# Where in the program a modulation's loads and sums are emitted: in the recurrence's chunks, or between projections and gates

## The chip, the cores and the metric

The kernel runs on one core of a Trainium2 chip. The metric is the time of one execution on the device in microseconds (us); of each kernel several runs are timed and the median counts. Five engines work side by side, each through its own queue and strictly in that queue's order: PE (TensorE, matrix products), DVE (VectorE), ACT (ScalarE), POOL (GpSimd) and SP (SyncE, which here only issues loads and stores). They wait for one another through semaphores. An instruction that waits holds up everything behind it on its own engine, and on no other.

## The reference, cut to what matters

One layer of a conditioned decoder for 512 tokens of 1024 channels, in float32:

```python
mod = c @ ada_w + ada_b                       # c: 1024 values, ada_w: 1024 x 6144
sh1, sc1, g1, sh2, sc2, g2 = split(mod, 6)
h = rmsnorm(x) * (1 + sc1) + sh1
z = h @ w_in                                  # -> attention | RWKV-7 | convolution | 3 gates
o_attn, o_rwkv, o_conv = attention(z_attn), rwkv7(z_rwkv), gated_conv(z_conv)
merged = sum(sigmoid(z_gate[i]) * (o[i] @ w_branch[i]) for i in range(3))
x = x + g1 * (merged @ w_o)
h = rmsnorm(x) * (1 + sc2) + sh2
x = x + g2 * ffn(h)
return rmsnorm(x)
```

The attention picks 128 keys for every query by an indexer's scores. The RWKV branch is a recurrence over tokens. Of the modulation, `sh1` and `sc1` are needed at once, for `h`. The other four parts, `g1`, `sh2`, `sc2` and `g2`, are needed only after `merged`: they are what is moved here.

## The kernel before, in words

**Products.** `h` is kept with channels on partitions, as a pair of parts (`h_hi`, `h_lo`). The columns of `w_in` are taken 128 at a time (`z_col`, line 402). Each such block is a load of 512 KB by SP (`load_raw`, L147, tile `wraw`, 4 buffers), a copy of its high part by ACT (`whi`, L163), the rest by POOL (`wlo`, L165; 3 buffers of each), and then 24 matmuls on PE (lines 177 to 179, below called column products) into one of three PSUM banks called `mm`. All 512 tokens run through each matmul. The RWKV branch has 14 of these blocks, 5 of them done early, the convolution 12, the attention 13 and then products with tokens on partitions (L188 to L190), the gates 24.

**The RWKV branch.** After its columns are there, four pairs of heads are prepared (L457 to L554; the last products on PE are those of L544 and L553). Then comes the substitution (L562 to L579): DVE alone inverts small triangular matrices in 31 steps, each a multiply (L569) and an add (L571) that needs the multiply. The matrices come in by the load `sub<-blk`, and the result goes through DRAM (`blk<-sub`, then four loads `Dm<-blk`, issued by ACT), is transposed by DVE (L579) and used by PE (L588, L591). Then the recurrence: 8 chunks of 64 tokens in turn (L602 to L650), a chain PE, DVE, PE, ACT, PE. Then a norm per head (L656 to L663, DVE), products that turn the result (L669), and the output of the branch.

**The rest up to the merge.** The convolution, the projections of the attention with the relative bias (masks `mk` on DVE, L721, products L727), the indexer's scores and the selection on DVE (L839 and L840, 32 rounds for each block of queries), the masked softmax for four pairs of heads (L855 to L897), and three branches of gates and branch products (`branch`, line 911). Then `w_o`, the second norm and the feed-forward part, which this change does not touch.

**The moved work.** `ada_parts` (line 196) is a Python generator. Each step loads one block of `ada_w` of 256 KB (tile `xraw`, three buffers) and adds it, times a column of `c`, to the tile `acc` on DVE: L215 for the first of eight blocks, L217 for the other seven. `finish` (line 199) sums a complete `acc` over the partitions with four one-column matmuls (L202) into an `mm` bank, and adds `ada_b` on DVE (L203). There are 64 steps in 8 groups of 8, and a last one that only finishes.

**What sets the order.** A tile framework with a scheduler writes the queue of each engine. It starts from the order in which the Python code emits the instructions, lets each engine run ahead by its own estimate of when operands are there, and respects the buffers. It may so place an instruction well before or after the place at which it was emitted. `with tc.high_priority` pulls the `whi` and `wlo` work forward. Memory comes from pools stacked from the left and from the right; a pool opened in a place used before waits, tile by tile, for the former users.

Of the kernel before, what the change touches and what calls it, by code (L numbers as in the profile page):

```python
# [19 lines left out]
D, S, MIX, DFF = 1024, 512, 512, 2816  # L20
# [39 lines left out]
def hybrid_block(ctx, tc, ins, out, consts, dbg=None, stop=99):  # L60
# [36 lines left out]
    start = right_pool("start")  # L97
# [52 lines left out]
    def weights(name, base, ld, k0, kt, cols, own=None, raw_own=None):  # L150
        """Rows 128*k0.. (kt blocks) and the columns [(start, width)..] of a row-major matrix with row length ld,
        as a pair of float32r tiles [128, kt, width] whose sum is the matrix."""
        wid = sum(n for _, n in cols)
        srcs, o = [], 0
        for c, n in cols:
            srcs.append(((lambda r, o=o, n=n: r[:, :, o:o + n]),
                         dram(name, base + k0 * 128 * ld + c, [[ld, 128], [128 * ld, kt], [1, n]])))
            o += n
        raw = load_raw([128, kt, wid], srcs, raw_own)
        pool, tag, bufs = (wp.pool, "w", 3) if own is None else (own[0], "x", own[1])  # L160
        with tc.high_priority(offset=4000):
            hi = pool.tile([128, kt, wid], F32R, name=tag + "hi", tag=tag + "hi", bufs=bufs)
            ACT.activation(hi, raw, AF.Copy)  # L163
            lo = pool.tile([128, kt, wid], F32R, name=tag + "lo", tag=tag + "lo", bufs=bufs)
            lo_engine[0].tensor_tensor(lo, raw, hi, op=ALU.subtract)  # L165
        return hi, lo
# [4 lines left out]
    def mm_t(ps, w, act, k0=0, start=True, stop=True):  # L171
        """ps += w^T @ act: the columns of w on partitions; act = (hi, lo) with channels on partitions."""
        hi, lo = w
        ahi, alo = act
        kt = hi.shape[1]
        for k in range(kt):
            PE.matmul(ps, hi[:, k, :], ahi[:, k0 + k, :], start=start and k == 0, stop=False)  # L177
            PE.matmul(ps, hi[:, k, :], alo[:, k0 + k, :], start=False, stop=False)  # L178
            PE.matmul(ps, lo[:, k, :], ahi[:, k0 + k, :], start=False, stop=stop and k == kt - 1)  # L179

    def mm_n(ps, act, tb, w, k0=0, start=True, stop=True):
        """ps += act^T @ w for the tokens of block tb (tokens on partitions)."""
# [13 lines left out]
    def ada_parts():  # L196
        """Parts 2.. of the modulation, half a part at a time: c_k * ada_w[k, 512 columns] summed over the eight row
        blocks, then over the partitions."""
# [28 lines left out]
    def rsqrt_of(v, n):  # L227
        """v^-1/2 of a small tile to full precision, in place: the table's root and one Newton step."""
        y = T("rsqt", [128, 32])[:, :n]
        ACT.activation(y, v, AF.Sqrt)  # L230
        DVE.reciprocal(y, y)
        DVE.scalar_tensor_tensor(v, v, -0.5, y, op0=ALU.mult, op1=ALU.mult)
        DVE.tensor_tensor(v, v, y, op=ALU.mult)
        DVE.scalar_tensor_tensor(v, v, 1.5, y, op0=ALU.add, op1=ALU.mult)
        return v

    def rsqrt_bits(v, n):
        """The same without a table: a first value from the bits of v, within 3.5 %, and three Newton steps, of which each
        squares the error."""
# [8 lines left out]
    def rstd_of(ss, n):  # L248
        """1/sqrt(ss/D + eps), in place."""
# [7 lines left out]
    def ada_first(c0, n):  # L257
        """Chunks c0..c0+n of the first two parts of the modulation, not yet summed over partitions."""
# [88 lines left out]
    def rel_pos(name, shape, aps, pos0, pool, keep=None):  # L347
        """Positions less the first one, in float32: exact however large they are, as long as the differences are exact."""
# [11 lines left out]
    def bias_operands():  # L360
# [16 lines left out]
        # scaled by a power of two to magnitudes under 2^15, and split into two parts of 11 bits  # L377
# [42 lines left out]
    def mixed(dst, i):  # L420
        """dst = z + (shift(z) - z) * mu for column block i of the branch."""
# [6 lines left out]
    # every sigmoid here is (1 + tanh(x / 2)) / 2, from the table that holds the exponential, too; lora_g, cs, a hold  # L428
    # twice the sigmoid, its running sum, and the tanh

    # unit u = pair * 8 + chunk; rows 0-63 / 64-127: the two heads of a pair, or for tokens
    # (own half q) U, L, N_b, B and (other half z) V, M, N_k, K
# [24 lines left out]
    for p in range(4):  # L457
# [51 lines left out]
        # V with tokens on partitions  # L509
# [10 lines left out]
        # products within the chunks  # L520
# [25 lines left out]
        # B and K, decayed to the chunk's end, with tokens on partitions  # L546
# [8 lines left out]
    ep.close()  # L555

    # (I - L)^-1: 32x32 diagonal blocks by substitution, one block per partition
# [42 lines left out]
    # the chunks in turn  # L600
    S_ = None
    for c in range(8):  # L602
        if c:
# [47 lines left out]
    # group norm per head and token, back to channels on partitions  # L651
# [35 lines left out]
    def conv3(dst, src, wts):  # L687
        """dst[t] = src[t-2] w0 + src[t-1] w1 + src[t] w2 along the free axis."""
# [17 lines left out]
    adp = left_pool("adp")  # L706
# [35 lines left out]
    # q, k and the indexer's as float32r pairs; row r of a block holds its high part, then its low part  # L742
# [46 lines left out]
    # A product of two 64-row operands in two passes: [q_hi; q_lo] with [k_hi; k_hi], then q_hi with k_lo. Heads of odd  # L789
    # number have the halves of the first operand swapped, so that q_hi lies where k_lo does.  # L790
    def load_q(dst, z, t0, n):
        """dst [128, 2, n]: the two heads of block z, tokens t0.."""
# [53 lines left out]
    # pT holds the transposed probabilities of both heads: key block b of the first in row b from column (b + 1) * 128,  # L846
    # that of the second in row 3 - b up to column (4 - b) * 128
# [62 lines left out]
    # merged holds twice the sum  # L910
# [42 lines left out]
    op_.close()  # L953
    adp.close()
    cvp.close()
    mid.close()

# [7 lines left out]
    def row_bc(c0, pool):  # L965
        """Modulation columns c0.. of modc as a row of 1024 on every partition."""
# [19 lines left out]
    def residual(x, hf, bank, row, ss):  # L986
        """x += row * (what the bank holds), and the sum of squares of the new values."""
# [14 lines left out]
    # Block rows of W^T: columns of a, columns of g. Blocks of the inner dimension: k < 512, k >= 512. Block columns of  # L1002
    # h: the two halves of the tokens.
# [7 lines left out]
    def pair(shape, src, ring=None):  # L1011
        """src as a pair of float32r tiles."""
# [36 lines left out]
    def product(ps, w, b, first):  # L1049
        """ps += w^T b over 512 rows."""  # L1050
# [20 lines left out]
    def h_block(c, th, dst):  # L1071
        """dst = h of channel block c, token half th."""
# [133 lines left out]
    # Inner blocks: the even and the odd channel blocks of f, pair by pair. Rows: the two halves of the tokens; columns:  # L1206
    # the two halves of the channels. First sweep: four products, each in its own banks; second sweep: the other three on
    # top of those, of which copies are kept.
# [15 lines left out]
    def w_tile(n, srcs):  # L1224
        """float32r pair [128, n, 512] of the sources, which fill it in turn."""
# [26 lines left out]
    def down(ps, i, a, ai, w, wi, first=False, last=False):  # L1252
        """ps += a^T w for the tokens of block i of a half."""
# [63 lines left out]
    def add_g2(tb, hf, v):  # L1317
        """x += g2 * v, v a half row in two pieces."""
# [8 lines left out]
    def high_half(tb):  # L1327
        """The columns of the second half, complete but for the norm's factor."""
# [92 lines left out]
```

## Time and profile before

| what | value |
|---|---|
| median of 3 runs | 1248.59 us (1246.18 to 1259.89) |
| the profiled execution, first to last instruction | 1246.3 us |
| PE busy, of that span | 1076.5 us (86%) |
| DVE busy | 945.3 us (76%) |
| ACT, POOL busy | 495.6 and 522.9 us |

The page gives the span of the profiled execution and no second time around it; the span lies within the three runs, 2.3 us under their median. A matmul's end is modelled, so a PE that the profile calls busy may still have room; the distance between the starts of two matmuls in a row is the safer measure. The granted clock (PEclk) is TensorE's, as a share of its full 2.4 GHz: 1.00 is full speed, and a mean between 0.5 and 1 says that part of the stretch ran at the lower level of 1.2 GHz. A wait is put down to the releaser that came last.

### The profile page before, as it was taken

To read this page: it belongs to the slowest core of one execution; us is meant where nothing else is said; L and a number is where in the kernel's file an instruction comes from. 1 tells how busy PE (TensorE), PEld (TensorE's weight loads), DVE (VectorE), ACT (ScalarE), POOL (GpSimd) and SP (SyncE) were. 2 spreads that over 40 slices of the span, in tenths; PEclk is the share of its full clock that TensorE was granted. 3 is DMA by queue.
4 is the path that set the end of the run, shared out by engine and by line. 5 is a ranking of instruction groups with operands and counts; after the bars stand their busy time and mean duration, and the time that the engine had idled before them with its cause. 6 is when DMAs were issued, how large, how long until landed. Compare 5 with 4: busy or idle time off the path is not lost.

```text
span 1246.3 us, 18485 instructions
## 1 busy us (share of the span) xinstructions
PE 1076.5 (86%) x6896; PEld 871.0 (70%) x6896; DVE 945.3 (76%) x1538; ACT 495.6 (40%) x890; POOL 522.9 (42%) x372
## 2 busy tenths in 40 slices
PE   4798999799999799888989999989888887679665
PEld 3676678577667768665666788889888886557444
DVE  6778777532789378976655444899898898999997
ACT  4243422242434244223434333665445454444442
POOL 3232223322222415554541000156566565776762
PEclk9789999899989899988999999989999999899898
DMA  9632123412348933698653535312323232244611
GB/s 313 174 86 71 39 60 102 95 35 66 107 150 253 303 96 86 193 235 218 179 134 98 145 101 166 115 51 85 92 79 101 73 99 85 76 170 168 218 53 68
DMA packets 194247, 156.97 MB, mean 126 GB/s; under 512 B 18499, under 2 KB 167389, under 8 KB 194157
## 3 DMA queue, kind: packets, MB, share of 16 engines
q1 hardware_dynamic: 165773, 131.22, 36.1%
q10 hardware_dynamic: 23056, 14.53, 3.9%
q0 software_dynamic: 5328, 10.03, 3.6%
q8 instruction: 54, 0.88, 0.3%
q14 instruction: 36, 0.29, 0.1%
HBM read 137.13 MB, written 18.63 MB: 125 GB/s over the span
## 4 chain that ended last, share of the span: by engine, by line
PE 39%; DVE 37%; issue 10%; DMA 6%; ACT 4%; POOL 2%; SPq 0%; ACTq 0%; DVEq 0%; POOLq 0%
PE mm L177 6%; PE mm L179 6%; PE mm L178 6%; DVE wlo L1237 3%; DMA xraw<-in_ada_w 3%; DVE acc L217 2%; DVE mg_lo L1250 2%; DVE h_lo L1046 2%; DVE slo L1237 2%; DVE slo L1017 2%; DVE acc L271 2%; PE sd L801 2%; DVE sub L571 1%; PE sd L727 1%; PE sd L800 1%
## 5 line engine op out<-in xcount | busy, mean ns | idle before, releaser
L165 POOL TENSOR_TENSOR wlo<-wraw,whi 128x1024 fp32r<-128x1024 f32 (+1 forms) x70 | 154.2, 2204 | 279.8 <-ACT whi L163 225.7
L178 PE MATMUL mm<-h_lo,whi 128*128 128x512 f32 (+2 forms) x496 | 201.8, 407 | 1.2 <-DVE h_lo L1082 1.2
L177 PE MATMUL mm<-h_hi,whi 128*128 128x512 f32 (+2 forms) x496 | 202.1, 408 | 0.7 <-DVE o_cv L702 0.7
L179 PE MATMUL mm<-h_hi,wlo 128*128 128x512 f32 (+2 forms) x496 | 201.3, 406 | 0.0
L163 ACT ACTIVATE whi<-wraw 128x1024 fp32r<-128x1024 f32 (+1 forms) x86 | 80.1, 934 | 222.2 <-PE mm L178 91.8
L178 PEld LDWEIGHTS mm<-h_lo,whi 128*128 128x128 f32 (+1 forms) x496 | 95.7, 193 | 23.5 <-issue 2.5
L177 PEld LDWEIGHTS mm<-h_hi,whi 128*128 128x128 f32 (+1 forms) x496 | 95.4, 193 | 22.4 <-issue 3.2
L179 PEld LDWEIGHTS mm<-h_hi,wlo 128*128 128x128 f32 (+1 forms) x496 | 95.6, 193 | 21.4 <-issue 1.5
L1053 PE MATMUL sd<-mg_hi,shi 128*128 128x256 f32 x240 | 70.1, 292 | 18.0 <-DVE p L1185 17.8
L1034 POOL TENSOR_TENSOR fS<-wraw 128x512 f32<-128x512 f32 x20 | 29.8, 1490 | 129.2 <-DMA wraw<-in_ffn_w_up 125.6
L217 DVE SCALAR_TENSOR_TENSOR acc<-xraw,ccol,acc 128x512 f32<-128x512 f32 x56 | 60.5, 1080 | 23.0 <-DMA xraw<-in_ada_w 22.5
L1055 PE MATMUL sd<-mg_hi,slo 128*128 128x256 f32 x240 | 68.1, 284 | 0.0
L1054 PE MATMUL sd<-mg_lo,shi 128*128 128x256 f32 x240 | 68.0, 283 | 0.0
L1017 DVE TENSOR_TENSOR slo<-fS,shi 128x1024 fp32r<-128x1024 f32 x40 | 60.5, 1512 | 0.5 <-ACT shi L1016 0.4
L1053 PEld LDWEIGHTS sd<-mg_hi,shi 128*128 128x128 f32 x240 | 45.9, 191 | 21.1 <-DVE p L1185 21.1
L1017 DVE TENSOR_TENSOR wlo<-wraw,whi 128x1024 fp32r<-128x1024 f32 x27 | 34.0, 1260 | 20.2 <-ACT whi L1016 20.1
L1053 PE MATMUL mm<-h_hi,whi 128*128 128x256 f32 x160 | 46.1, 288 | 3.0 <-ACT p L1066 3.0
L721 DVE TENSOR_SCALAR mk<-posq,thr 128x512 f16<-128x512 f32 (+3 forms) x128 | 44.7, 421 | 4.1 <-PE sd L727 4.1
L1016 ACT ACTIVATE shi<-fS 128x1024 fp32r<-128x1024 f32 x40 | 42.1, 1052 | 10.7 <-PE sd L1054 10.5
L1054 PEld LDWEIGHTS sd<-mg_lo,shi 128*128 128x128 f32 x240 | 46.0, 192 | 0.0
L1055 PEld LDWEIGHTS sd<-mg_hi,slo 128*128 128x128 f32 x240 | 45.9, 191 | 0.0
L1054 PE MATMUL mm<-h_lo,whi 128*128 128x256 f32 x160 | 45.6, 285 | 0.0
(565 smaller groups left out, 3120.6 us busy)
## 6 DMA issues: line engine op xcount, KB each, us to landing
wraw<-in_w_in SPq DMA_DIRECT2D x61, 512.0 KB, 4.1
xraw<-in_ada_w SPq DMA_DIRECT2D x96, 256.0 KB, 4.2
wraw<-in_ffn_w_up SPq DMA_DIRECT2D x44, 512.0 KB, 3.8
wraw<-in_ffn_w_down SPq DMA_DIRECT2D x17, 512.0 KB, 3.5
wraw<-in_w_branch SPq DMA_DIRECT2D x24, 256.0 KB, 3.6
bias_d<-stage ACTq DMA_DIRECT2D x10, 512.0 KB, 5.8
wraw<-in_w_o SPq DMA_DIRECT2D x8, 512.0 KB, 3.8
h_hi<-in_ffn_w_down SPq DMA_DIRECT2D x8, 512.0 KB, 4.5
```

The lines of the kernel that those rows point to most:

```text
L163: ACT.activation(hi, raw, AF.Copy)
L165: lo_engine[0].tensor_tensor(lo, raw, hi, op=ALU.subtract)
L177: PE.matmul(ps, hi[:, k, :], ahi[:, k0 + k, :], start=start and k == 0, stop=False)
L178: PE.matmul(ps, hi[:, k, :], alo[:, k0 + k, :], start=False, stop=False)
L179: PE.matmul(ps, lo[:, k, :], ahi[:, k0 + k, :], start=False, stop=stop and k == kt - 1)
L217: DVE.scalar_tensor_tensor(acc, raw, ck, acc, op0=ALU.mult, op1=ALU.add)
L721: DVE.tensor_scalar(m_[:, :n], posq[:, b * 128:], thr[:, b, gg:gg + 1], None, op0=ALU.is_ge)
L1017: DVE.tensor_tensor(lo, src, hi, op=ALU.subtract)
L1053: PE.matmul(ps, at(w[0], k), b[0][:, k], start=first and k == 0, stop=False, skip_group_check=True)
L1054: PE.matmul(ps, at(w[0], k), b[1][:, k], start=False, stop=False, skip_group_check=True)
L1055: PE.matmul(ps, at(w[1], k), b[0][:, k], start=False, stop=k == 3, skip_group_check=True)
L1237: DVE.tensor_tensor(lo[:, d], src, hi[:, d], op=ALU.subtract)
```

## The change

Five steps of the generator are taken at the head of each of the 8 chunks, 40 of the 64, which before were taken in `branch`. The four steps between the attention's key projections stay, and `branch` takes what is left. So that the tiles exist, the pool `adp` is opened after the RWKV preparation instead of after the convolution, and closed after the convolution's pool instead of before it. Comments and docstrings are gone as well, which computes nothing and shifts line numbers by one to three from here on.

```diff
     ep.close()
+    adp = left_pool("adp")
     sp = right_pool("sp")
 ...
     S_ = None
     for c in range(8):
+        for _ in range(5):
+            next(ada)
         if c:
             px = sd_bank()
 ...
     tap("o_conv", o_cv)
-    adp = left_pool("adp")
     bi = right_pool("bi")
 ...
     mg.close()
     op_.close()
-    adp.close()
     cvp.close()
+    adp.close()
     mid.close()
```

What the scheduler makes of it is seen in the queues. First SP, from the loads of the recurrence's first weights on. `wraw` are column weights, `xraw` the modulation's blocks. Before:

```order
L147 DMA wraw<-in_w_in 128x8x128 x3
L373 DMA rb<-in_rel_bias 128x1x8
L374 DMA rb<-in_rel_bias 124x1x8
L147 DMA wraw<-in_w_in 128x8x128 x22
L147 DMA wraw<-in_w_in 128x8x72
L147 DMA wraw<-in_w_in 128x8x128 x3
L755 DMA z_att<-wk 128x512
```

And with the change:

```order
L374 DMA rb<-in_rel_bias 124x1x8
L147 DMA wraw<-in_w_in 128x8x128 x13
L147 DMA xraw<-in_ada_w 128x512 x44
L147 DMA wraw<-in_w_in 128x8x128
L147 DMA xraw<-in_ada_w 128x512 x4
L147 DMA wraw<-in_w_in 128x8x128
L147 DMA xraw<-in_ada_w 128x512 x3
L147 DMA wraw<-in_w_in 128x8x128 x7
L351 DMA posqi<-in_positions 128x512
```

Forty-four modulation loads now stand between the sixteenth and the seventeenth of the column weights, and seven more close behind.

Second, DVE at the start of the substitution. Before, between its steps stand operations of the convolution (L690 and others):

```order
L563 MEMSET sub 128x1024
L564 MEMSET sub 128x32
L569 TENSOR_TENSOR st<-sub 128x31
L698 TENSOR_TENSOR wk<-wk,mm 128x512
L571 TENSOR_TENSOR sub<-sub,st 128x31
L569 TENSOR_TENSOR st<-sub 128x60
L571 TENSOR_TENSOR sub<-sub,st 128x30x2
L569 TENSOR_TENSOR st<-sub 128x87
L690 SCALAR_TENSOR_TENSOR wk<-wk,cw 128x511
```

With the change (L570 and L572 are the multiply and the add):

```order
L564 MEMSET sub 128x1024
L565 MEMSET sub 128x32
L215 TENSOR_SCALAR acc<-xraw,ccol 128x512
L570 TENSOR_TENSOR st<-sub 128x31
L217 SCALAR_TENSOR_TENSOR acc<-xraw,ccol,acc 128x512
L572 TENSOR_TENSOR sub<-sub,st 128x31
L217 SCALAR_TENSOR_TENSOR acc<-xraw,ccol,acc 128x512
L570 TENSOR_TENSOR st<-sub 128x60
L572 TENSOR_TENSOR sub<-sub,st 128x30x2
L570 TENSOR_TENSOR st<-sub 128x87
L572 TENSOR_TENSOR sub<-sub,st 128x29x3
L217 SCALAR_TENSOR_TENSOR acc<-xraw,ccol,acc 128x512
```

It goes on like this: of the modulation's 64 sums, 38 stand among the 62 steps of the substitution and ten between its end and the last of the transposes L580. So the scheduler did not put them into the chunks, at whose heads they are emitted, but before them. The other 16 stand in the selection for the last block of queries; none stands in the softmax, which had 24 before.

Third, PE and ACT right behind the preparation of the last pair of heads. On PE before, column products follow at once; there are 183 of them from here to the first L588:

```order
L553 MATMUL sd<-ident,BK 128x128 x3
L544 MATMUL sd<-UV,LM 64x64 x7
L553 MATMUL sd<-ident,BK 128x128 x5
L179 MATMUL mm<-h_hi,wlo 128x512
L177 MATMUL mm<-h_hi,whi 128x512
```

With the change (buffer numbers kept), four `finish` of the modulation come first, and then 60 column products up to the first L589:

```order
L553 MATMUL sd_1459<-ident_70,BK_1302 128x128 x4
L202 MATMUL mm_1803<-one_66,acc_1691 128x1 x4
L202 MATMUL mm_1926<-one_66,acc_1741 128x1 x4
L202 MATMUL mm_2003<-one_66,acc_1864 128x1 x4
L202 MATMUL mm_2126<-one_66,acc_1941 128x1 x4
L177 MATMUL mm_2309<-h_hi_93,whi_2305 128x512
```

The fourth of them reads the `acc` that is complete with sum 32. On ACT, the store of the substitution's result, `blk<-sub`, now follows the load of its input directly, ahead of the next `whi`; before, five `whi` stood between the two:

```order
L554 ACTIVATE HYL<-sd 128x4x2x64 x2
L563 DMA sub<-blk 128x1024
L574 DMA blk<-sub 128x1024
L163 ACTIVATE whi<-wraw 128x1024
L699 ACTIVATE wk<-mm 128x512
L576 DMA Dm<-blk 32x32x32
```

In all of the program's queue on PE, the column products that stand ahead of some marks are, before and with the change: first L588/L589 416 and 276; first product of the head norm (L669/L672) 623 and 432; first product of the indexer (L821/L823) 816 and 816; first transposition of the softmax (L885/L887) 1185 and 1108; its last product (L894/L896) 1433 and 1331; all 1872 and 1872.

## Rows read from the trace of the kernel before

**Rows 1.** Windows: busy us (count) of each engine, granted clock, DMA share.
```profile
core 0: us, PE busy (x) PEld busy (x) DVE busy (x) ACT busy (x) POOL busy (x), PEclk, DMA share, GB/s
186.00:230.00 44.00, 42.89 (x183) 33.85 (x181) 35.25 (x67) 9.86 (x13) 14.90 (x6) 1.00 0.31 85
237.00:247.00 10.00, 10.00 (x36) 7.74 (x34) 4.86 (x4) 1.06 (x1) 4.62 (x2) 0.74 0.57 122
256.00:312.00 56.00, 55.53 (x607) 43.25 (x602) 18.66 (x37) 16.75 (x35) 12.25 (x10) 1.00 0.19 54
341.00:425.00 84.00, 79.73 (x928) 62.35 (x926) 68.91 (x160) 30.16 (x60) 26.26 (x16) 0.96 0.77 226
425.00:441.00 16.00, 11.40 (x80) 11.11 (x81) 0.75 (x1) 3.74 (x5) 5.73 (x4) 0.79 0.98 240
441.00:548.00 107.00, 100.82 (x416) 75.20 (x415) 98.68 (x200) 38.53 (x66) 52.31 (x35) 0.97 0.49 140
548.00:688.00 140.00, 124.64 (x531) 88.13 (x530) 81.58 (x185) 53.07 (x127) 56.62 (x45) 0.94 0.66 164
688.00:745.00 57.00, 57.00 (x249) 46.10 (x248) 26.55 (x35) 21.34 (x30) 2.94 (x4) 1.00 0.47 128
```

**Rows 2.** Groups by line, DVE, 191 to 232: busy, mean ns, idle before.
```profile
L571 DVE TENSOR_TENSOR sub<-sub,st 128x31 f32<-128x31 f32 (+15 forms) x31 | 19.0, 614 | 0.9
L569 DVE TENSOR_TENSOR st<-sub 128x31 f32<-128x31 f32 (+15 forms) x31 | 10.6, 341 | 6.6 <-DMA sub<-blk 5.7
```

**Rows 3.** Timeline (start us, us), POOL and DVE in the substitution.
```profile
199.35 0.30 DVE L571 TENSOR_TENSOR sub<-sub,st 128x135 f32<-128x135 f32 x1
...
199.79 2.47 POOL L165 TENSOR_TENSOR wlo<-wraw,whi 128x1024 fp32r<-128x1024 f32 x1 [3.16 <-ACT whi L163]
200.04 2.40 DVE L571 TENSOR_TENSOR sub<-sub,st 128x156 f32<-128x156 f32 x1
```

**Rows 4.** Timeline, first and last of the substitution's 62 steps on DVE.
```profile
191.74 0.19 DVE L569 TENSOR_TENSOR st<-sub 128x31 f32<-128x31 f32 x1 [5.69 <-DMA sub<-blk]
...
230.97 0.19 DVE L571 TENSOR_TENSOR sub<-sub,st 128x31 f32<-128x31 f32 x1
```

**Rows 5.** Source line L217: duration in ns min/median/max, first and last start.
```profile
L217 DVE SCALAR_TENSOR_TENSOR acc<-xraw,ccol,acc x56: 726/752/2882, 377.9 to 627.6; 128x512 f32<-128x512 f32 x56
```

**Rows 6.** DMA view 335 to 380 (median us to landing); then tile `xraw`.
```profile
xraw<-in_ada_w SPq DMA_DIRECT2D x5, 256.0 KB, 3.4
...
DMA to landing us min/median/max: 2.7/4.1/9.0
```

**Rows 7.** Timeline, one sum on DVE and the load that its buffer lets go.
```profile
377.88 0.73 DVE L217 SCALAR_TENSOR_TENSOR acc<-xraw,ccol,acc 128x512 f32<-128x512 f32 x1
...
378.64 0.33 SPq L147 DMA_DIRECT2D xraw<-in_ada_w  x1
```

**Rows 8.** Timeline of PE around the substitution, and the head norm's first product.
```profile
185.20 0.77 PE L553 MATMUL sd<-ident,BK 128*128 128x128 f32 x5
...
236.83 0.39 PE L588 MATMUL sd<-Dm,LG 32*32 32x32 f32 x4 [7.21 <-DMA Dm<-blk]
...
242.57 0.40 PE L177 MATMUL mm<-h_hi,whi 128*128 128x512 f32 x1
242.81 0.40 PE L178 MATMUL mm<-h_lo,whi 128*128 128x512 f32 x1
...
329.18 1.03 PE L669 MATMUL sd<-ident,MV 64*64 64x64 f32 x28 [2.21 <-DVE MV L663]
```

**Rows 9.** Timeline of DVE, first operation of the head norm.
```profile
312.04 2.29 DVE L656 TENSOR_REDUCE gn<-MV 128x32 f32<-128x2048 f32 x1 [2.98 <-ACT MV L648]
```

**Rows 10.** Waits in 548 to 640, PE's and DVE's: total us, times, longest.
```profile
PE sd L885 <- DVE lg L881: 10.9, 7, 3.5
...
DVE acc L217 <- DMA xraw<-in_ada_w: 14.0, 7, 4.7
```

**Rows 11.** Groups by line, DVE, 500 to 548: busy, mean ns, idle before.
```profile
L217 DVE SCALAR_TENSOR_TENSOR acc<-xraw,ccol,acc 128x512 f32<-128x512 f32 x20 | 25.2, 1262 | 0.0
```

More of the change, by code (lines that the diff above doesn't have):

```diff
@@ L953, in hybrid_block @@
     op_.close()
+    cvp.close()
     adp.close()
-    cvp.close()
     mid.close()
```

## The prediction, made before the changed kernel's time was known

> **What bounds the kernel now.** I read the span first, then the table of windows, then the waits and the lines of the windows that the change touches. In the windows [rows 1] the reader is to see that PE has next to no idle time from the end of the RWKV preparation to the merge: 42.89 of 44 us busy in 186 to 230, while DVE does the substitution; 55.53 of 56 in the recurrence; 79.73 of 84 in the attention's projections; 57.00 of 57 in the gates. Room on PE there is only in 425 to 441 (11.40 of 16), in the selection (441 to 548: 100.82 of 107, with DVE at 98.68, so both are near their limit) and in the softmax (548 to 688: 124.64 of 140, at a clock of 0.94). PE can be busy for all this time because the column products depend on nothing but weights, and the queue always has some to put in the gaps of the RWKV work. One such product costs 0.234 us (42.89 us for 183 [rows 1]; the next two in a row start 0.24 apart [rows 8]); I use 0.233. So the question is where the change leaves PE without such products.
>
> **What the change does.** It adds no arithmetic: 64 loads, 64 sums, the finishes and all 1872 column products are there before and after. It moves them. By the queues the sums do not land in the recurrence's chunks: 38 of 64 stand among the 62 steps of the substitution, before the recurrence. And two engines are tied to them. PE meets four finishes right behind the preparation, the fourth of which needs sum 32, and everything behind it on PE waits too. ACT meets the store of the substitution's result before the next `whi`, so that no new weights can be made until the substitution is over.
>
> **How long the sums take there.** Two rates compete. The ring: three `xraw` buffers, so three loads per round. A load is issued 0.03 us after the sum that frees its buffer has ended (377.88 + 0.73 = 378.61, issue 378.64 [rows 7]); it lands after 3.4 us (a median of five loads; over all loads 2.7 to 9.0, median 4.1 [rows 6]); the sum takes 0.75 [rows 5]. Together 4.18 us for three sums. DVE's own work: the steps took 19.0 + 10.6 = 29.6 us [rows 2]. In these are four stalls such as the one at 200.04, where a POOL `wlo` runs and a step of 0.30 us takes 2.40 [rows 3]; at 2.1 us each they are some 8.5. With them out, and 0.04 us between operations, a step is 23.6 / 62 = 0.38 us. Since ACT makes no `whi` in this stretch, POOL has no `wlo`, and the stalls go (if they stayed: 8.5 us on top). Three sums and the 4.9 steps that go with them are 3 x 0.75 + 4.9 x 0.38 = 4.1 us. The two rates are nearly equal and each will sometimes wait for the other: I take 4.3 us per three sums. Bounds: landings of 2.7 leave 4.1 (2 us less in all), landings of 4.1 give 4.9 (6.6 us more).
>
> The Trainium skill, page "DMA: Bandwidth & Descriptors", section "Anatomy of one DMA — SWDGE (gpsimd) path", gives a fixed 2.0 us and bytes over 436 GB/s for one transfer; for 256 KB that is an estimate of 2.6 us, fitted on another path than SP's. The trace does not agree: 3.4 in the median [rows 6]. By the page the ring would be 3.4 us, DVE would set the rate alone, and the sum below would be 2 us less.
>
> **PE's silence.** The substitution starts at 191.74 [rows 4] with the first sums in it. The load of sum 5 is issued at the end of sum 2, about 192.7, so sum 5 starts at 196.2; sum 32 follows nine rounds later at 196.2 + 9 x 4.3 = 234.9, and PE, which was done with the preparation at 186.0 (185.20 + 0.77 [rows 8]), goes on at 236. That is 50 us of silence, where 43 us of products were done before. Sum 38 comes at 243.5 and the last step at 244.8, not 231 [rows 4]: 13.6 us later.
>
> **From there to the selection.** PE does the 60 products that it has, 14.0 us, plus 2.6 us for a clock that will be low after the silence (after a wait of 7.2 us [rows 8] the next 10 us were granted 0.74 [rows 1]): 252.6. The result of the substitution needs 5.7 us to reach PE (231.16 to 236.83 [rows 4, 8]), to 250.7, which these products hide. Twelve more products, 2.8 us, and the recurrence is where it stood before at about 242.3 [rows 8]: 13 us late. In the recurrence PE is full [rows 1] and has about seven products fewer, 1.5 us. So the head norm's first product, at 329.18 before [rows 8], comes 11.5 us late. By then PE has done 432 column products instead of 623. The 191 missing ones are the loss itself: 191 x 0.233 = 44.5 us. DVE's head norm, 17 us from 312.04 [rows 8, 9], has no products left to cover it, which costs another 2.6 us of clock behind it; its idle time is not counted twice, since it is part of the 191. Against that stands idle time that the late products can fill: 84 - 79.73 = 4.3 us in 341 to 425 and 16 - 11.40 = 4.6 in 425 to 441, where the DMA share of 0.98 [rows 1] falls, as 51 modulation loads have left. The selection so starts 11.5 + 44.5 + 2.6 - 8.9 = 49.7 us late, with the same 816 products done.
>
> **From the selection to the merge.** The selection keeps 16 sums and loses 8, at 1.26 us each there [rows 11]: -10.1. The softmax loses its 24 sums, and 25 products (-5.8 us). Its PE waits for `lg` were 10.9 us, while DVE itself stood 14.0 us at sums whose loads were late [rows 10]; I let half of these waits go (-5.5), and half of the clock lost behind them (140 x 0.06 = 8.4 [rows 1]; -4.2). But 541 products instead of 439 then stand behind the softmax, where PE is full [rows 1]: 102 x 0.233 = +23.8. Together -1.8. Loads and sums that stay in the attention cost what they did.
>
> **The sum** is 49.7 - 1.8 = +47.9 on the profiled execution's 1246.3, 1294 us. That execution lies 2.3 us under the median of 1248.59, within the three runs.
>
> **The rivals.**
> *Mild.* The silence is as long, but the later stretches give more back: all idle time of 441 to 688 (6.2 + 15.4 us) and all clock lost there (107 x 0.03 + 140 x 0.06 = 11.6) go, since DVE is relieved and PE has products enough; 33.2 us instead of 1.8: 1263 us. For it: DVE is at 98.68 of 107 in the selection. Against it: the softmax gets fewer products to fill its gaps, not more. Chance 0.21.
> *Heavy.* Landings are 4.1 us as in the median over all loads, because column weights and modulation share the queue (+6.6), and the projections absorb nothing (+8.9): 1310; without the late savings on waits and clock (9.7) 1319. Chance 0.14.
> *The other side.* Not PE but DVE with its late loads bounds the attention. Then the 8 sums that leave the selection (8 x 1.26 [rows 11]), the 24 that leave the softmax (24 x 0.75 [rows 5]) and its 14.0 us at late loads [rows 10] go entirely, 42 us, while the substitution pays 13.6: 1246 - 42 + 14 = 1218. For it: the 14.0 us at late loads [rows 10]. Against it: PE is full before 425 and after 688 [rows 1], and the lost products must be done at some time. It decides if PE's silence stays below about 30 us, which would take sum 32 at 216, two us per three sums, while three sums alone take 2.25 [rows 5]. Chance 0.03.
> *Nothing.* The scheduler's queues differ, but idle time before and after is equal: PE's silence would have to be filled, which strict queue order excludes unless the finishes do not block. Chance 0.04.
>
> **How the numbers follow.** The forecast of 1294 has 0.58. Its own bounds are -2 and +6.6 from the ring, some +8.9 from what isn't absorbed. The range takes in the mild case and the heavy one: 1260 to 1318. One per cent, 12.5 us, is what a measurement of this kernel can tell from no change. Faster by more than that has 0.04, within it 0.05, slower 0.91: the mild rival is slower by 14 us, and a milder one still may fall within.
>
> **What would show it.** Right: PE idle for about 50 us from 186 with DVE as its releaser at the finishes (L202), and a lower clock behind it; DVE's waits in the substitution for loads of `xraw`, steps spread over some 53 us instead of 39; no POOL `wlo` and no 2.4 us steps in it; the head norm's first product about 11 us late with PE idle ahead of it; the selection's start about 50 us late; no sums in the softmax; a longer stretch from the softmax to the merge. Wrong: PE doing products between 190 and 230; a substitution under 45 us; sums in the chunks after all; or a softmax and selection shorter by 30 us.

## The result, and the profile after

The changed kernel takes 1299.31 us in the median of four runs (1289.98 to 1306.24), the kernel before 1249.78 beside it (1246.18 to 1259.89). The ratio is 1.0376, 95% interval 1.0308 to 1.0443: 3.8% slower. The profiled execution is the longest of the four, with a span of 1304.5 us, 58.2 more than before. The four runs scatter over 16 us, so the terms below, which come from the two traces, sum to 58.2 and not to the 49.5 between the medians. Medians and ranges are over all runs of a kernel; the ratios leave out runs in a slower state at a lower clock, which several kernels here show, the one before among them.

First the windows of the changed kernel, in the columns of [rows 1]: the substitution, the recurrence, the head norm, the end of the attention's projections, the selection, the softmax, and the gates.

```profile
186.00:236.00 50.00, 10.38 (x39) 9.53 (x40) 39.06 (x92) 0.08 (x1) 0.00 (x0) 0.53 0.60 184
265.00:321.00 56.00, 54.85 (x651) 42.79 (x645) 18.82 (x37) 17.18 (x35) 13.14 (x10) 1.00 0.14 38
321.00:345.00 24.00, 14.04 (x156) 9.51 (x154) 15.66 (x23) 5.51 (x6) 2.35 (x1) 0.79 0.20 56
430.00:478.00 48.00, 47.30 (x410) 42.45 (x409) 17.75 (x50) 14.44 (x23) 20.69 (x17) 1.00 0.81 216
478.00:602.00 124.00, 108.56 (x386) 76.66 (x384) 88.95 (x201) 36.64 (x65) 49.40 (x37) 0.83 0.45 113
602.00:721.00 119.00, 105.94 (x425) 71.98 (x424) 61.29 (x136) 47.44 (x118) 56.60 (x42) 0.90 0.46 115
721.00:800.00 79.00, 79.00 (x343) 63.84 (x342) 32.90 (x44) 27.11 (x40) 4.24 (x5) 1.00 0.38 111
```

PE is all but silent during the substitution, 10.38 of 50 us busy where it had been 42.89 of 44 [rows 1], and POOL runs no `wlo` there. Then, from the timeline of PE, the places of [rows 8]:

```profile
184.00 0.77 PE L553 MATMUL sd<-ident,BK 128*128 128x128 f32 x5
198.29 1.86 PE L202 MATMUL mm<-one,acc 128*128 128x1 f32 x8 [13.52 <-DVE acc L217]
...
231.22 1.84 PE L202 MATMUL mm<-one,acc 128*128 128x1 f32 x8 [9.81 <-DVE acc L217]
232.91 0.77 PE L177 MATMUL mm<-h_hi,whi 128*128 128x512 f32 x1
...
249.00 0.31 PE L589 MATMUL sd<-Dm,LG 32*32 32x32 f32 x4
...
335.78 1.97 PE L672 MATMUL sd<-ident,MV 64*64 64x64 f32 x32 [9.96 <-DVE MV L666]
...
348.05 0.50 PE L177 MATMUL mm<-h_hi,whi 128*128 128x512 f32 x1 [1.94 <-DVE o_cv L705]
```

The releaser in the brackets of the L202 is the sum (L217); two more such waits lie between, and the four make 40.9 us. This much is as forecast. The groups of DVE in 186 to 250 answer to [rows 2]:

```profile
L217 DVE SCALAR_TENSOR_TENSOR acc<-xraw,ccol,acc 128x512 f32<-128x512 f32 x38 | 29.1, 764 | 4.3 <-DMA xraw<-in_ada_w 3.9
L572 DVE TENSOR_TENSOR sub<-sub,st 128x31 f32<-128x31 f32 (+15 forms) x31 | 10.5, 338 | 0.4
```

A step's add has 338 ns in the mean instead of 614. What the prediction had not looked at is when DVE writes the convolution's output, `o_cv`. The line of `o_cv` in the changed kernel, and then in the kernel before (duration in ns, first and last start):

```profile
L705 DVE TENSOR_TENSOR o_cv<-wk,mm x4: 678/680/687, 347.3 to 369.4; 128x512 f32<-128x512 f32 x4
```

```profile
L702 DVE TENSOR_TENSOR o_cv<-wk,mm x4: 678/684/690, 203.1 to 279.2; 128x512 f32<-128x512 f32 x4
```

And DVE's timeline of the changed kernel around the first of them:

```profile
346.71 0.69 DVE L678 SCALAR_TENSOR_TENSOR o_rw<-yg,sd 128x512 f32<-128x512 f32 x1
347.31 1.88 DVE L705 TENSOR_TENSOR o_cv<-wk,mm 128x512 f32<-128x512 f32 x3
```

Three of the four writes of `o_cv` come in one go, directly behind the very last operation of the RWKV branch, 144 us later than before. Each of them reads an `mm` bank. So three convolution blocks were complete and held all three `mm` banks, and no column product could start behind them until the RWKV branch had ended: the next one, at 348.05, was released by `o_cv`. In the changed kernel this stop came late. Behind the silence PE was full (54.85 of 56 us in 265 to 321), the last of its 432 column products began at 325.4, and only the 9.96 us of idle time ahead of the head norm, and the 1.94 at 348.05, are the stop's.

The marks of all kernels, first starts in us except for the softmax's last product, all of PE but `o_cv`; the last column is the span:

| kernel | first with `Dm` | `o_cv` | head norm | indexer | softmax | its last product | span |
|---|---|---|---|---|---|---|---|
| before | 236.8 | 203.1 | 329.2 | 441.6 | 568.1 | 688.0 | 1246.3 |
| changed | 249.0 | 347.3 | 335.8 | 478.2 | 601.7 | 721.0 | 1304.5 |
| pool_only | 246.6 | 349.3 | 336.9 | 480.2 | 613.0 | 736.7 | 1291.8 |
| dummy6 | 235.7 | 202.3 | 327.7 | 441.7 | 533.6 | 644.2 | 1319.1 |
| dummy8 | 239.7 | 346.9 | 334.5 | 477.8 | 558.2 | 668.5 | 1348.3 |
| two_per_chunk | 247.1 | 351.9 | 340.4 | 482.8 | 636.9 | 749.4 | 1316.5 |
| fit | 255.7 | 272.7 | 343.9 | 471.8 | 600.3 | 719.9 | 1309.7 |
| sd_finish | 244.6 | 356.5 | 343.8 | 487.4 | 593.3 | 717.9 | 1312.1 |
| sd_fit | 244.8 | 208.9 | 351.9 | 455.3 | 565.7 | 688.2 | 1284.9 |
| sd_fit_in_chunks | 236.0 | 202.3 | 349.6 | 452.0 | 555.8 | 680.3 | 1273.9 |
| pool_fit | 245.3 | 205.4 | 337.6 | 441.8 | 574.2 | 711.9 | 1281.1 |
| omit40 | 238.2 | 204.7 | 330.1 | 441.4 | 550.1 | 663.7 | 1238.3 |
| spread2 | 238.4 | 204.6 | 330.1 | 441.4 | 549.0 | 676.0 | 1251.4 |

From before to changed the table gives +36.6 us up to the indexer, -3.0 over the selection, -0.6 over the softmax and +25.2 behind it.

### The profile page after: what moved, and what is told of

The parts are those of the page before. It is cut to its first block, busy times and chain, and to the rows that moved or that the text cites. A ratio compares the mean times of both kernels' runs of the same rounds, so it can differ in the third digit from the quotient of the medians.

```text
span 1304.5 us, 18478 instructions
## 1 busy us (share of the span) xinstructions
PE 1091.9 (84%) x6896; PEld 883.6 (68%) x6896; DVE 938.9 (72%) x1538; ACT 495.6 (38%) x890; POOL 518.8 (40%) x372
## 4 chain that ended last, share of the span: by engine, by line
PE 43%; DVE 32%; issue 10%; DMA 8%; ACT 4%; POOL 3%; SPq 0%; DVEq 0%; ACTq 0%; POOLq 0%
PE mm L177 8%; PE mm L179 8%; PE mm L178 8%; DMA wraw<-in_ffn_w_up 3%; DVE wlo L1239 3%; DVE mg_lo L1252 2%; DVE h_lo L1048 2%; DMA xraw<-in_ada_w 2%; DVE slo L1019 2%; DVE slo L1239 2%; PE sd L803 2%; DVE acc L217 2%; PE sd L802 1%; DVE wlo L1019 1%; PE sd L729 1%
## 5 line engine op out<-in xcount | busy, mean ns | idle before, releaser
L723 DVE TENSOR_SCALAR mk<-posq,thr 128x512 f16<-128x512 f32 (+3 forms) x128 | 53.8, 489 | 5.2 <-PE sd L729 5.2
L202 PE MATMUL mm<-one,acc 128*128 128x1 f32 x64 | 13.0, 324 | 50.1 <-DVE acc L217 50.1
L217 DVE SCALAR_TENSOR_TENSOR acc<-xraw,ccol,acc 128x512 f32<-128x512 f32 x56 | 48.2, 861 | 6.3 <-DMA xraw<-in_ada_w 5.8
L202 PEld LDWEIGHTS mm<-one,acc 128*128 128x128 f32 x64 | 12.8, 293 | 51.5 <-DVE acc L217 31.5
L876 DVE CUSTOM_DVE_ANT_0 lg<-sd,bt 128x128 f32<-128x128 f32 (+3 forms) x32 | 15.3, 489 | 44.6 <-PE sd L803 41.9
```

The lines of the kernel that those rows point to most:

```text
L217: DVE.scalar_tensor_tensor(acc, raw, ck, acc, op0=ALU.mult, op1=ALU.add)
L723: DVE.tensor_scalar(m_[:, :n], posq[:, b * 128:], thr[:, b, gg:gg + 1], None, op0=ALU.is_ge)
```

## The experiments

Two theories were set against each other. The **silence** theory is the prediction's: sums in the substitution, with finishes ahead of PE's products, cost the products of that time. The **place** theory came from `o_cv`: the change also opens the pool `adp` earlier, and everything opened behind it lies 10 KB per partition higher (three `xraw` and two `acc` of 2 KB each). `o_cv` is among it, and so lies on tiles that the recurrence and the head norm still use.

**The early pool alone (pool_only).** The changed kernel without the steps in the chunks:

```diff
     for c in range(8):
-        for _ in range(5):
-            next(ada)
```

> The pool adp is opened early, as in the change, but no step is emitted in the chunks: branch takes the 40 steps as before. Silence theory (the loss is PE waiting at the finishes for sums in the substitution): the finishes stand on PE where they stood before the change, so PE does not wait, and the time is that of the kernel before, 1246 to 1256 us. Place theory (the early pool pushes o_cv, the convolution's output, onto the recurrence's tiles, so that o_cv is first written after the head norm, 347 us instead of 203, and three convolution blocks hold all mm banks until then): 432 column products are done at the head norm as in the changed kernel, instead of 623; 191 x 0.233 = 44.5 us less some 8 to 10 that later idle time absorbs, 1275 to 1290 us, with PE idle within the recurrence instead of within the substitution.

Measured: 1293.43 us (1292.7 to 1295.38), ratio 1.0342 (1.029 to 1.0395). No step is emitted in the chunks, and nearly all of the loss is there. 16 sums still run ahead into the substitution. PE is 47.25 of 60 us busy from 186 to 246, has done all 432 products by then, and has none left for the recurrence. The window of the recurrence and the norm, columns as above, and PE's longest wait in 186 to 480 (total us, times, longest):

```profile
246.00:337.00 91.00, 61.23 (x741) 54.53 (x741) 26.11 (x47) 16.76 (x34) 6.06 (x7) 0.52 0.06 13
```

```profile
PE sd L670 <- DVE MV L664: 14.9, 1, 14.9
```

The DMA share is 0.06: no weights are loaded, since nothing consumes them. The granted clock is 0.52, almost all of it at the lower level, while PE did the recurrence's small products only; with column products between them it was 1.00 [rows 1].

**A dead pool of 6 and of 8 KB in the kernel before (dummy6, dummy8).** The modulation's steps are where they were, and the two kernels differ in the size of the pool alone, and so in the place of `o_cv`:

```diff
     ep.close()
+    dmp = left_pool("dmp")
+    POOL.memset(T("dummy", [128, KB * 256], pool=dmp.pool)[:, 0:1], 0.0)
 ...
     cvp.close()
+    dmp.close()
```

> The kernel before, with a pool of 6 KB per partition that nothing uses, opened where the change opens adp and kept until the merge. o_cv lies 6 KB higher and still clear of the recurrence's tiles: 623 products at the head norm as before, and the sums stand where they stood. Later, merged finds no room beside the softmax, so that no gates run ahead (948 products at the softmax's last product instead of 1433): slower than before by some of 485 x 0.233 = 113 us, 1300 to 1350 us. What counts is the difference to the pool of 8 KB. Up to the indexer both theories expect the times of the kernel before, first indexer product at 441 us.

> The same with 8 KB: o_cv now overlaps the recurrence's lowest tiles by 1.5 KB; 432 products at the head norm instead of 623; no other difference to 6 KB up to there, and the same queue order behind it. Place theory: first indexer product 28 to 40 us later than with 6 KB, and the whole time longer by as much. Silence theory, by which the sums in the substitution and the finishes ahead of the products make the loss: no sum is moved here, so at most 5 us between the two.

Measured: 1317.93 us (1307.62 to 1323.53) and 1350.31 (1346.37 to 1365.7), on the same chip. The 2 KB cost 32 us, and the indexer starts at 441.7 and 477.8: the difference of 36.1 us is the change's 36.6. With 6 KB `o_cv` is written as early, and PE is as full in the recurrence, as in the kernel before:

```profile
L704 DVE TENSOR_TENSOR o_cv<-wk,mm x4: 678/685/690, 202.3 to 277.7; 128x512 f32<-128x512 f32 x4
```

```profile
250.00:312.00 62.00, 61.53 (x717) 47.93 (x717) 21.80 (x39) 20.36 (x40) 14.63 (x11) 1.00 0.21 56
```

With 8 KB:

```profile
L704 DVE TENSOR_TENSOR o_cv<-wk,mm x4: 673/678/679, 346.9 to 370.2; 128x512 f32<-128x512 f32 x4
```

```profile
250.00:312.00 62.00, 50.71 (x552) 45.20 (x554) 12.87 (x29) 11.18 (x26) 4.44 (x7) 0.51 0.04 10
```

So the place by itself is enough for this loss, whatever the sums do. Both kernels are slow for another reason besides, which is the same in the two: only 948 column products, not 1433, are done at the softmax's last product.

**Fewer steps per chunk (two_per_chunk).** `range(5)` becomes `range(2)`.

> The change with two steps per chunk instead of five: 24 sums stand in the substitution instead of 38, fewer finishes are waited for ahead of the products, 369 products instead of 276 at the first product with Dm, but o_cv is placed as in the change, and 432 products stand ahead of the head norm again. Place theory: the number at the head norm decides, not the silence: first indexer product at 475 to 485 us as with five steps and with none, and 1285 to 1300 us in all. Silence theory: the loss goes with the length of PE's wait, about half of it: 1268 to 1280 us.

Measured: 1310.16 us (1301.08 to 1320.95), ratio 1.0403 (1.0297 to 1.0509). PE's wait at the finishes is 13.2 us instead of 40.9, and the indexer still starts at 482.8, as the place theory has it. The total is above the silence theory's range, and by its ratio (1300 us) at the upper end of the place theory's: here 38 sums stand in the selection, which takes 154 us instead of 126.5. While `o_cv` is late, the length of the silence does not set the loss up to the indexer.

**`o_cv` free, the silence kept (fit).** One `acc` instead of two, and `Xs` in the space of `st`, make 4 KB per partition:

```diff
-            acc = T("acc", [128, 512], pool=adp.pool, bufs=2)
+            acc = T("acc", [128, 512], pool=adp.pool, bufs=1)
 ...
-            Xs = X("Xs", [128, 4, 64], bufs=2)
+            Xs = X("Xs", [128, 4, 64], tag="st")
```

> The changed kernel with 4 KB less beside the recurrence (one acc instead of two, and Xs kept in the space of st), so that o_cv fits beside the recurrence's tiles; the sums stay in the substitution and the finishes stay ahead of the products on PE. Silence theory: PE is idle from about 186 to 230 as in the changed kernel, 477 products at the head norm instead of 432 give back 45 x 0.233 = 10 us: 1285 to 1295 us. Place theory: with o_cv free the silence is made up in the recurrence, 1250 to 1262 us.

Measured: 1314.65 us (1311.44 to 1323.88), ratio 1.0522 (1.0445 to 1.0598). Both theories missed it, the place theory by over 50 us. `o_cv` is first written at 272.7, and PE still waits 42.5 us at the finishes. Its window from the silence to the head norm:

```profile
237.00:345.00 108.00, 103.80 (x1037) 81.72 (x1037) 49.83 (x83) 30.31 (x50) 29.53 (x17) 0.98 0.32 82
```

PE is full behind the silence (103.80 of 108) and can't make it up. So the silence is a cause as well: it alone leaves 477 products at the head norm, and the place of `o_cv` alone 432. The two don't add up, since both withhold the same products: with both the indexer is 36.6 us late, with the silence alone 30.2. (The single `acc` may add to these 30.2: the first product with `Dm` comes at 255.7 instead of 249.0.) The other half of this kernel's loss, 31.5 us, lies behind the softmax, at whose last product it has done 1283 column products instead of 1433.

**No silence, `o_cv` late (sd_finish).** The finish takes a bank of the ring that the recurrence uses:

```diff
-            pm = mm_bank()
+            pm = sd_bank()
```

> The changed kernel with one word changed: finish takes one of the five sd banks instead of one of the three mm banks, so that its place in the ring of banks is behind the recurrence's chunks and not ahead of the convolution. o_cv still lies on the recurrence's tiles. 16 sums stay in the substitution, 31 go between its end and the head norm. Silence theory: no wait of PE in the substitution, 1245 to 1258 us. Place theory: 432 products at the head norm as in the changed kernel, now with the idle time in the recurrence: 1275 to 1290 us.

Measured: 1297.48 us (1296.67 to 1313.82), ratio 1.0403 (1.0307 to 1.05). By the code, with `mm` the finishes come ahead of the convolution in the order in which the three banks are given out; with `sd` PE waits at no finish in the substitution and is 40.46 of 49 us busy in it (186 to 235). The loss stays, 7 us above the place theory's upper end and 40 above the silence theory's, and the indexer starts 9 us later still than in the changed kernel.

**Both edits (sd_fit).**

> Both edits: finish in sd banks, and o_cv free of the recurrence's tiles. 671 products at the head norm (623 before the change), 32 sums between the substitution and the head norm, none in selection and softmax. Both theories: neither cause is left, so at most 1250 us; with 48 products more at the head norm (11 us) and no sum in the selection, 1225 to 1250. If instead sums cost their time wherever they stand in a chain of DVE, the recurrence (56 us before) gets longer by up to 32 x 0.75 = 24 us, and the time is 1255 to 1275.

Measured: 1286.65 us (1278.31 to 1287.54), ratio 1.0271 (1.0205 to 1.0337). Neither cause is left, and up to the indexer 13.7 us of the 36.6 remain: from the first product with `Dm` to the head norm 107.1 us pass instead of 92.4. Not all of this is delay, for PE does 237 column products in this stretch instead of 207 (30 x 0.233 = 7.0 us), beside 32 sums on DVE and four finishes. The selection, with no sum in it, is 16.1 us shorter, but behind the softmax 38.4 us are lost: 90 products more are left to do there (21 us), and 24 sums and their finishes stand there, at which PE waits 7.7 us.

**The sums truly in the chunks (sd_fit_in_chunks).** Both edits, and the five sums of a chunk queued on DVE behind that chunk's copy of `UV`:

```diff
-        for _ in range(5):
-            next(ada)
 ...
-        DVE.tensor_copy(UV[0:64, :, c, 0, :], pu3[0:64])
+        u_ = DVE.tensor_copy(UV[0:64, :, c, 0, :], pu3[0:64]).ins
+        with tc.issue_after(u_):
+            for _ in range(5):
+                next(ada)
```

> The version in which the sums stand in the chunks: finish in sd banks, o_cv clear of the recurrence's tiles, and the five sums of a chunk queued on DVE behind that chunk's copy of UV. No sum in the substitution, 35 between it and the head norm, 5 to the selection, 24 behind the softmax. Place and silence theory: no cause of the change's loss is left, 1246 us or under. Chain theory: each sum on DVE delays the recurrence's chain: the stretch from the first product with Dm to the head norm's first product, 92.4 us before, 107.1 in the version with both edits alone, gets 10 to 25 us longer than before, and 1340 products instead of 1433 at the softmax's end leave 21 us for the tail: 1275 to 1295 us.

Measured: 1275.87 us (1271.86 to 1279.8), ratio 1.0197 (1.0135 to 1.0259). This is what the change's words say, and it is slower too. Up to the indexer it loses 10.4 us, in the selection, now without sums, it wins 22.7, and behind the softmax it loses 35.3, with 90 products more to do there as in sd_fit. From `Dm` to the head norm 113.6 us pass instead of 92.4, which is in the chain theory's range. The groups of DVE in 236 to 350, and the window of this stretch:

```profile
L217 DVE SCALAR_TENSOR_TENSOR acc<-xraw,ccol,acc 128x512 f32<-128x512 f32 x35 | 34.1, 975 | 2.5 <-DMA xraw<-in_ada_w 2.0
```

```profile
236.00:349.60 113.60, 105.92 (x1030) 82.16 (x1030) 75.06 (x107) 33.33 (x55) 33.23 (x19) 0.97 0.61 178
```

The 21 us are not all the sums' doing. PE is 105.92 of 113.60 us busy and does 260 column products instead of 207, which is 53 x 0.233 = 12.3 us; some 9 us are left for 40 sums and four finishes. Two runs without any column product in this stretch, both at a clock of 0.52, agree: it took 90.3 us without a sum (pool_only) and 99.2 with 32 sums and four finishes (sd_finish). So sums in the recurrence do lengthen it, but by about a quarter of a microsecond each, finishes included; how this splits between the two no run shows.

**The early pool with `o_cv` free (pool_fit).** pool_only with the two edits of fit.

> The early pool alone, no step in the chunks, but with the 4 KB less that let o_cv lie clear of the recurrence's tiles (one acc, Xs in the space of st). Against the early pool without these 4 KB (1293 us) only o_cv's place and the number of acc differ. Place theory: 638 products at the head norm (623 before the change), first indexer product at 438 to 446 us, total 1245 to 1260 us. If it is the early pool in some other way (its eight sums in the substitution, its addresses): 1275 to 1295 us.

Measured: 1282.03 us (1270.49 to 1282.83), ratio 1.0173 (1.008 to 1.0266). The mark that tells the theories apart came out as the place theory said: the indexer at 441.8 instead of 480.2. The total did not, by 22 us: 5.9 us are lost in the selection, 17.8 in the softmax, where 29 sums now stand between the marks of the table instead of 16, and 10.9 behind it. With one `acc`, each group of sums must wait for the finish of the one before; that this is what moved the sums is likely but not shown. PE's largest wait in 186 to 760 (total us, times, longest):

```profile
PE sd L885 <- DVE lg L881: 22.5, 10, 5.8
```

**What is there to gain (omit40).** The kernel before with the generator's groups cut from eight to three.

> The kernel before, with 40 of the 64 loads and sums and five of the eight finishes left out altogether: it does less than the reference asks, and its time is the bound on what any place for these 40 can bring. Prediction's view (the sums cost 1.26 us each in the selection, and the softmax's waits for lg are half theirs): 1225 to 1236 us. Chain view (the softmax is bound by its own chain PE, DVE, ACT, DVE, PE, since in the changed kernel it took 119.5 us without a sum and 119.8 with 24): 1240 to 1248 us.

Measured: 1244.37 us (1238.77 to 1266.66), ratio 0.9913 (0.9885 to 0.9941). 40 loads and sums less bring 0.9%, by the ratio 1239 us, between the two views. The selection is 17.8 us shorter and the softmax 6.3, but 16.3 are lost behind it, since 72 products fewer are done by then (16.8 us). So this is the time of the queue that the scheduler wrote for less work, and a guide to what there is to win rather than a strict bound. None of the 24 sums that are left stands in the softmax, and PE waits for `lg` there as much as ever (550 to 664; total, times, longest):

```profile
PE sd L887 <- DVE lg L883: 14.6, 11, 2.8
```

**Thinner steps in the gates (spread2).** Two or three `next(ada)` behind a gate instead of four, pools as before.

> The kernel before, with its pools as they were, but the steps in branch thinner: two behind each gate of the first branch and three behind each of the others, instead of four: 16 of the 64 sums move from selection and softmax behind the softmax, where DVE is 26.55 of 57 us busy. Leaving 40 steps out brought 0.9%, so at most half of that is to be had: 1240 to 1250 us beside 1253 of the kernel before. If instead the 1374 products at the softmax's last product (1433 before) cost 59 x 0.233 = 14 us in the tail without a shorter softmax: 1255 to 1265.

Measured: 1253.29 us (1244.15 to 1270.95), ratio 1.0014 (0.9965 to 1.0063): no difference. No version that does all of the work beats the kernel before, and by omit40 there is little to win.

## Why the prediction was right, and where it was not

The time was forecast as 1294, 5 us under the median, and the direction and the likeliest case held. The mechanism held by half: it names one of two causes, each of which is enough, and the terms behind it are off in ways that partly cancel.

**How long the sums take: right.** Three sums took 4.07 us (from sum 5 at 193.72 to sum 32 at 230.32, nine rounds) where 4.3 was taken; the last step of the substitution stood at 240.44, 9.5 us later than before, where 13.6 was forecast; PE's first product came at 232.91, not 236. The stalls behind POOL did go: the add of a step fell from 614 to 338 ns with no `wlo` in the stretch. The Trainium skill, page "SBUF — State Buffer", section "Summary: rules for kernel authors", says that of a DVE operation with two inputs in SBUF and a GpSimd operation that reads SBUF, the second to issue is held until the first has finished. The step of 2.40 us against 0.30 [rows 3], and these 338 ns, agree.

**The 191 missing products at the head norm: the number right, the cause told by half.** The prediction calls them "the loss itself" and puts them down to "PE's silence", "where 43 us of products were done before". The silence came as forecast, and in the changed kernel it is where PE's time went: 40.9 us of waits at the finishes, against 9.96 us ahead of the head norm. With `o_cv` free it still costs 30.2 us of the 36.6 up to the indexer (fit). What does not hold is that the loss hangs on it: with a third of the silence or none it is 36 to 41 us (two_per_chunk, pool_only, and dummy8, in which no step is moved), since 432 is also what `o_cv`'s place allows. The prediction counted the products per mark in the queue and took the count for a result of the sums. The queue holds both causes, so the right count was no proof of the one named; the line of the diff that opens `adp` earlier was passed over.

**From the head norm to the indexer: mis-sized.** 44.5 + 2.6 - 8.9 = 38.2 us were forecast, and 30.0 measured (142.4 instead of 112.4). The 191 products are there (384 instead of 193 in this stretch), but more was absorbed than the 8.9: PE's idle time fell from 8.9 to 2.7 us, and the kernel before had also lost clock, with 0.96 in 341 to 425 and 0.79 in 425 to 441 [rows 1]. In 430 to 478 the changed kernel was granted 1.00, and PE is 47.30 of 48 us busy. With 5 us less at the head norm than forecast (+6.6, not +11.5), the indexer was 36.6 us late, not 49.7.

**Selection and softmax: wrong, and it hid the error above.** -10.1 and -15.5 were forecast, with the border between them at 548, and -3.0 and -0.6 measured, with the border at the softmax's first transposition; together -25.6 and -3.6. In the softmax the changed kernel has no sum of the modulation, and PE's waits for `lg` there are 12.9 us; in the kernel before, between the same marks, 11.3:

```profile
PE sd L887 <- DVE lg L883: 12.9, 8, 4.7
```

So these waits are there without any sum: the softmax's own chain through DVE and ACT makes them, and 25 products fewer gave nothing back. In fit, too, the softmax takes 119.6 us with no sum, against 119.9 before. This holds for the order of these kernels only: with 29 sums in the softmax (pool_fit) it took 137.7 us, and the waits for `lg` were 22.5.

**The tail: right.** 23.8 forecast for 102 products, 25.2 measured, at a PE that is 79.00 of 79 us busy.

**The rivals.** The mild case would have needed 33 us back in selection and softmax; 3.6 came. "Nothing" and the faster case fell with the first mark. The heavy case supposed landings of 4.1 us and no absorption: the changed kernel's 96 `xraw` loads landed in 3.1 us in the median, and more than the 8.9 us was absorbed. That the forecast time came out so close is partly luck: 13 us too much up to the indexer and 22 us too much relief behind it cancelled but for some 10 us, so that +47.9 stands against +58.2 between the traces and +49.5 between the medians.

**Open.** Why the selection gave back only 3.0 us with half its sums (16 instead of 32 between its marks) and 77 column products fewer: its clock was 0.83, and PE waited 9.3 us there at finishes. That sums and finishes cost time there is seen in sd_finish, sd_fit and sd_fit_in_chunks, where it took 104 to 110 us with neither, at about as many column products (303 instead of 292). How the price splits, no run separates.

## What to carry to other kernels

When work is emitted earlier, its memory moves earlier too: look at which tile is pushed onto one still in use, and whose banks wait behind it. A tile's first write, before and after, shows this in one line, and a dead pool of two sizes tests it without touching the work. When two causes withhold the same work, taking one away gives little back: each must be tested alone as well. Before moving work off a busy stretch, leave it out once: the time without it says about how much any place can bring.

## What the runs showed of the hardware

In this kernel the recurrence is no faster when the column products between its own are left out, and the granted clock is lower then: without any it took 90.3 us from the first product with `Dm` to the head norm at a clock of 0.52 (pool_only), and 92.4 in the kernel before, with 207 of them at 0.97. What the column products would cost the recurrence at an equal clock no run shows.
